# Feed-forward activations transposed by VectorE blocks and two DMAs instead of on TensorE, and a bucket table written 32 times instead of 128

## The chip, the cores and the metric

The kernel runs on one core of a Trainium2 chip. The metric is the device time of one execution in microseconds; lower is better. The trace was taken by the hardware profiler from one execution, and its times count from the first instruction of that execution.

## The reference, cut to what matters

Two transformer blocks run one after the other on one sequence of 256 tokens with 2048 features, in float32. Each ends in a gated feed-forward of width 5632 (the first block's `D_FF` and the second's `D_FF_2`), and these two are what the change touches, besides a bias of the second block's attention:

```python
# first block
gate, up = jnp.split(h @ w_gate_up[layer], 2, axis=-1)
x = x + rms_norm((jax.nn.silu(gate) * up) @ w_down[layer], g_ffn_post[layer])

# second block: a causal convolution of width 3 over the tokens, for each of 2 * 5632 columns
def conv_ffn(h, w_up, conv_w, conv_b, w_down):
    L = h.shape[1]
    u = h @ w_up
    up = jnp.pad(u, ((0, 0), (CONV_WIDTH - 1, 0), (0, 0)))
    acc = conv_b
    for j in range(CONV_WIDTH):
        acc = acc + conv_w[j] * up[:, j:j + L]
    gate, val = jnp.split(acc, 2, axis=-1)
    return (jax.nn.silu(gate) * val) @ w_down

# second block's attention: a bias for each head from the bucket of the distance
dist = t_pos[None, :, None] - sel
bias = t5_table[t5_bucket(jnp.maximum(dist, 0))]
```

## The kernel before

**Matmuls.** Every weight matrix is cut into chunks of 512 output columns, and a chunk into half pieces of 256 rows (512 KB). The 256 tokens are two tiles `t` of 128. A product is made of three float32r passes: activation high part by weight high part (A), high by low (B), low by high (C). So a half piece and a tile make 6 matmuls of 128x128 by 128x512, all issued in `step` (line 331). A chunk over 2048 rows has 8 half pieces and 96 matmuls. Its result stands with tokens on the partitions, in one PSUM bank of the class `mm` for each tile.

**Weights.** SyncE loads a half piece into a staging page (line 254), ScalarE casts it into the high part (line 278), VectorE subtracts for the low part (line 285). Casts are issued up to 12 planned us ahead of the piece's first matmul (`AHEAD_HI`), low parts 11 (`AHEAD_LO`).

**Order.** One Python loop (`run`) writes out the order of the whole program: it walks the matmul steps with a planned clock of 0.216 us for a matmul, and issues loads, casts and low parts as they come due. What happens after a chunk (its `done`) is a generator. All generators move by one tick for every 1.4 planned us (`TICK`, `pump`), and `yield n` sleeps n ticks. Ticks only set the place of an instruction in its engine's queue; each engine works through its queue in order and waits where an operand is missing.

**Memory.** SBUF is 25 pages of 128x2048 floats (`PAGES`), shared by weights (`ring`, `stg`), whole pages (`s8`) and quarter pages of 128x512 (`s2`, at most 4 pages). PSUM has 4 banks of the class `mm` and 4 of `sd`. The DMAs of the generators go out on GpSimd's queue (`mq`), the weight loads on SyncE's.

**First feed-forward** (`ffn`, 11 blocks of 512 columns in parts of two). A gate chunk leaves silu(gate) in a quarter page (`ffn_gate`). After the up chunk, `ffn_up` multiplies PSUM by it on VectorE (line 1017), sleeps 1 + 2 ticks, transposes the 128x512 result on TensorE in four squares into an `sd` bank (line 346), and `evac_split` makes the high part on ScalarE (line 352) and the low part on VectorE (line 353), feature-major, for the down chunks. Chunks of part g + 1 stand ahead of the down chunks of part g, so a block is finished well before it is read, except for the last one: between its up chunk and its own down part stand only the four down chunks of the part before.

**Second feed-forward** (`ffn2`, same order). After each gate or value chunk `two` scales the two tiles out of PSUM on ScalarE (line 1214), and after 3 ticks `conv` transposes them on TensorE, two groups of four squares a tick apart (line 1534), so that tokens lie along the free dimension. On each of four 128x256 pieces ScalarE applies the first tap and the bias (line 1541) and VectorE the two others (lines 1542 and 1543), reading the `sd` bank. A gate's result gets its silu (line 1546). After a value chunk GpSimd multiplies gate by value (line 1560), ScalarE makes the high part (line 1563) and GpSimd the low part (line 1564).

**Bucket table.** `prep_t5`, started at the second gate chunk of the first feed-forward, forms for 8 heads the 512 bias values by distance, with the heads on eight partitions, and writes each head's row 128 times to DRAM (line 490). Much later `topk` reads it with a row step of 511 (line 1284), so that each partition gets a row shifted by one: one DMA for each token tile.

Of the kernel before, what the change touches and what calls it, by code (L numbers as in the profile page):

```python
# [8 lines left out]
F32 = mybir.dt.float32  # L9
# [9 lines left out]
P = 128  # L19
# [17 lines left out]
B_STEP = 2  # L37
LO_LAG = 2
NEG = -1.0e30
EPS = 1e-6  # L40
# [39 lines left out]
class Core:  # L80
# [267 lines left out]
    def evac_split(self, bank, hi, lo, scale=None):  # L348
# [5 lines left out]
        else:  # L354
            nc.scalar.activation(hi, bank, AF.Copy, scale=scale)
            nc.vector.scalar_tensor_tensor(lo, bank, scale, hi.bitcast(F32), op0=ALU.mult, op1=ALU.subtract)

    def x_block(self, src, xt, j, t, goff):

        nc = self.nc  # L360
        if xt.blk[j] is None:
            xt.blk[j] = True
            xt.blk[j] = yield from self.get("s8", dt=F32R)
        while xt.blk[j] is True:
            yield 1
        bank = yield from self.get("sd")
        self.transposes(bank, [src[:, a * P : (a + 1) * P] for a in range(4)])
        g = [self.cols[:, goff + 4 * j + a : goff + 4 * j + a + 1] for a in range(4)]
        b3 = bank.rearrange("p (k n) -> p k n", k=4)
        s = slice(t * P, (t + 1) * P)  # L370
        hi, lo = xt.hi(j)[:, :, s], xt.lo(j)[:, :, s]
        for a in range(4):
            nc.scalar.activation(hi[:, a], b3[:, a], AF.Copy, scale=g[a])  # L373
        xt.ready_hi.add((j, t))

        def low():
            yield LO_LAG
            for a in range(4):
                nc.vector.scalar_tensor_tensor(lo[:, a], b3[:, a], g[a], hi[:, a].bitcast(F32), op0=ALU.mult, op1=ALU.subtract)  # L379
            self.put("sd")  # L380
            xt.ready.add((j, t))

        self.spawn(low())
# [12 lines left out]
    def consts(self):  # L396
# [22 lines left out]
        self.d_lb = d.tile([2, 1024], F32, name="d_lb")  # L419
        self.d_t5 = d.tile([8, P, 512], F32, name="d_t5")  # L420

# [57 lines left out]
    def prep_t5(self):  # L479
        nc, i = self.nc, self.i  # L480
        hot, w = yield from self.get("s2", 2)
        bank = yield from self.get("sd")
        self.mq.dma_start(hot[0:32, :], i["c_hot"])
        self.mq.dma_start(w[0:32, 0:8], i["t5"])
        yield 6
        nc.tensor.matmul(bank[0:8, :], w[0:32, 0:8], hot[0:32, :], start=True, stop=True)
        yield 2
        nc.scalar.copy(w[0:8, :], bank[0:8, :])
        self.put("sd")
        self.mq.dma_start(self.d_t5, w[0:8, None, :].to_broadcast([8, P, 512]))  # L490
        self.drop(hot, w)
        self.flags.add("t5")
# [516 lines left out]
    def ffn_up(self, c, i):  # L1009
# [3 lines left out]
        def done(t):  # L1013
# [5 lines left out]
            a = self.act[i]  # L1019
            yield 1  # L1020
            if a.blk[0] is None:
                a.blk[0] = True
                a.blk[0] = yield from self.get("s8", dt=F32R)
            while a.blk[0] is True:
                yield 1
            yield 2
            bank = yield from self.get("sd")
            self.transposes(bank, [g[:, b * P : (b + 1) * P] for b in range(4)])
            self.drop(g)
            s = slice(t * P, (t + 1) * P)  # L1030
            self.evac_split(bank.rearrange("p (k n) -> p k n", k=4), a.hi(0)[:, :, s], a.lo(0)[:, :, s])
            self.put("sd")
            a.ready.add((0, t))
# [240 lines left out]
    def topk(self):  # L1274
# [7 lines left out]
        for t in range(2):  # L1282
            n = P * (t + 1)
            self.mq.dma_start(bias[t], bass.AP(tensor=self.d_t5.tensor, offset=self.d_t5.offset + 255 - P * t,
                                               ap=[[511, P], [P * 512, 8], [1, n]]))
        for t in range(2):
# [237 lines left out]
    def conv(self, c, i, gate):  # L1524
# [3 lines left out]
        def then(got):  # L1528
            outs = []
            for a in range(2):  # L1530
                bank = yield from self.get("sd")
                for b in range(2):
                    for t in range(2):
                        nc.tensor.transpose(bank[:, (2 * b + t) * P : (2 * b + t + 1) * P],  # L1534
                                            got[t][:, (2 * a + b) * P : (2 * a + b + 1) * P], self.ident)
                o = yield from self.get("s2")
                for b in range(2):
# [5 lines left out]
                    nc.vector.scalar_tensor_tensor(v[:, 2:], u[:, 0:254], w[0], v[:, 2:], op0=ALU.mult, op1=ALU.add)  # L1543
                self.put("sd")
                if gate:
# [3 lines left out]
                yield 1  # L1549
            self.drop(got[0], got[1])  # L1550
            if gate:
# [415 lines left out]
def _layout(np, a):  # L1967
# [5 lines left out]
    def cols(v):  # L1973
        return v.reshape(-1, 128).T

    conv_w = a["conv_w_2"][0]
    vectors = [a["g_mix_pre"][0], a["g_ffn_pre"][0], a["g_ple_pre"][0], a["norm1_g_2"][0], a["norm2_g_2"][0],
               a["kv_norm_g_2"][0], a["hgrn_gnorm"][0], a["conv_b_2"][0], conv_w[0], conv_w[1], conv_w[2]]
    r = {
# [8 lines left out]
        "w_gu": _pieces(np, a["w_gate_up"][0]),  # L1988
        "w_dn": _pieces(np, a["w_down"][0]),
        "w_pg": _pieces(np, a["w_ple_gate"][0]),  # L1990
# [6 lines left out]
        "w_up2": _pieces(np, a["w_up_2"][0]),  # L1997
        "w_dn2": _pieces(np, a["w_down_2"][0]),
        "g_mix_post": a["g_mix_post"][0], "g_ffn_post": a["g_ffn_post"][0], "g_ple_post": a["g_ple_post"][0],
# [20 lines left out]
```

## Time and profile before

| | |
|---|---|
| three runs | 2699.81, 2703.37, 2704.06 us; median 2703.37 |
| the profiled execution | 2698.83 us, span of its instructions 2696.8 us |
| TensorE, matmuls | 2656.7 us busy, 99% |
| VectorE | 1559.6 us, 58% |
| ScalarE | 1310.5 us, 49% |
| GpSimd | 312.5 us, 12% |
| weight queue (SyncE) | 476.83 MB, 51.0% of the 16 DMA engines' time |
| GpSimd's DMA queue | 34.50 MB, 4.2% |

Busy time is the time in which an engine had at least one instruction under way. Matmuls overlap, so the mean duration of one (392 ns at line 331) is longer than the distance between two starts. A group of the trace is named by line, engine, operation and operands; "idle before" is the engine's idle time just ahead of the group's instructions, with what ended it. A line can be that of a helper: line 346 serves all callers of `transposes`.

### The profile page before, as it was taken

The page shows a single profiled execution, that of the slowest core. Times are in us where ns is not written, and L with a number is a line of the kernel's source. Part 1 is how long each engine was busy: PE and PEld are TensorE (multiplying, and loading weights), DVE is VectorE, ACT ScalarE, POOL GpSimd, SP SyncE. Part 2 cuts the span into 40 slices and gives each one's busy share as a digit, 9 for nine tenths or more (in the row PEclk, how much of TensorE's full clock was granted, in tenths as well). Part 3 has the DMA queues.
Part 4 walks back from the last instruction along what each step waited for, and adds up shares of the span by engine and source line. Part 5 has one row for each costly group of instructions (what it writes and reads, how often), then busy time and mean ns, then how long its engine had stood idle before and what let it go on. Part 6 is the DMA issues. An engine that isn't in the chain of part 4 may idle for free. (4 is left out here: it accounts for less than half of the span.)

```text
span 2696.8 us, 32408 instructions
## 1 busy us (share of the span) xinstructions
PE 2656.7 (99%) x12193; PEld 2194.9 (81%) x12193; DVE 1559.6 (58%) x2063; ACT 1310.5 (49%) x1916; POOL 312.5 (12%) x298
## 2 busy tenths in 40 slices
PE   8999999999999999999999999999999999999998
PEld 7887788888778888888887778788888888888887
DVE  6865675465635445454557564855555646464656
ACT  6545644454525443434345564555455535353634
POOL 1341031021200000000002310100001101020101
PEclk9999999999999999999999999999999999999999
DMA  7445446667576555555557555455555555555553
GB/s 252 164 144 165 152 154 200 218 230 262 197 182 227 191 195 193 193 197 193 192 176 241 206 211 179 146 178 198 187 181 189 185 189 185 190 194 181 195 180 132
DMA packets 144539, 513.97 MB, mean 191 GB/s; under 512 B 17688, under 2 KB 20272, under 8 KB 143360
## 3 DMA queue, kind: packets, MB, share of 16 engines
q1 hardware_dynamic: 133504, 476.83, 51.0%
q0 software_dynamic: 9584, 34.50, 4.2%
q8 instruction: 95, 1.56, 0.2%
q10 hardware_dynamic: 1296, 0.59, 0.1%
q14 instruction: 60, 0.49, 0.1%
HBM read 497.16 MB, written 14.70 MB: 190 GB/s over the span
## 5 line engine op out<-in xcount | busy, mean ns | idle before, releaser
L331 PE MATMUL mm<-ring,s 128*128 128x512 f32 (+1 forms) x10824 | 2526.3, 392 | 4.1 <-ACT s L373 4.1
L331 PEld LDWEIGHTS mm<-ring,s 128*128 128x128 f32 x10824 | 2018.8, 188 | 424.2 <-issue 7.1
L285 DVE TENSOR_TENSOR ring<-stg,ring 128x1024 fp32r<-128x1024 f32 x896 | 1090.7, 1263 | 477.8 <-ACT ring L278 469.4
L278 ACT CAST ring<-stg 128x1024 fp32r<-128x1024 f32 (+1 forms) x904 | 905.1, 1050 | 186.0 <-PE mm L331 68.0
L352 ACT CAST s<-sd 128x512 fp32r<-128x512 f32 (+2 forms) x56 | 28.9, 516 | 225.7 <-PE sd L346 187.9
L1214 ACT ACTIVATE s<-mm,ss 128x512 f32<-128x512 f32 x60 | 41.5, 692 | 198.7 <-PE mm L331 186.0
L1051 DVE TENSOR_TENSOR s<-mm,s 128x512 f32<-128x512 f32 x72 | 48.9, 688 | 107.8 <-PE mm L331 107.8
L1560 POOL TENSOR_TENSOR s<-s,s 128x512 f32<-128x512 f32 x22 | 40.5, 1841 | 583.1 <-DVE s L1543 583.1
L1541 ACT ACTIVATE s<-sd,cols 128x256 f32<-128x256 f32 x88 | 48.6, 563 | 96.0 <-DVE s L1543 61.8
L1542 DVE SCALAR_TENSOR_TENSOR s<-sd,cols,s 128x255 f32<-128x255 f32 x88 | 42.4, 482 | 83.0 <-ACT s L1541 82.4
L1017 DVE SCALAR_TENSOR_TENSOR s<-mm,ss,s 128x512 f32<-128x512 f32 x22 | 16.4, 750 | 110.6 <-PE mm L331 110.6
L1004 ACT ACTIVATE s<-mm,ss 128x512 f32<-128x512 f32 x22 | 15.2, 691 | 132.0 <-PE mm L331 130.8
L346 PE MATMUL sd<-ident,s 128*128 128x128 f32 x340 | 54.6, 284 | 21.3 <-DVE s L975 7.2
L346 PEld LDWEIGHTS sd<-ident,s 128*128 128x128 f32 x340 | 43.2, 146 | 36.1 <-issue 10.2
L353 DVE TENSOR_TENSOR s<-sd,s 128x512 fp32r<-128x512 f32 (+2 forms) x56 | 33.9, 605 | 65.6 <-ACT s L352 65.6
L1064 POOL DMA_DIRECT2D s<-in_p_dram x2 | 1.1, 550 | 603.8 <-PE mm L331 603.8
L799 POOL TENSOR_TENSOR s<-s,s 128x512 f32<-128x512 f32 x32 | 53.1, 1668 | 94.0 <-ACT s L796 89.3
L373 ACT ACTIVATE s<-sd,cols 128x128 fp32r<-128x128 f32 x160 | 45.7, 383 | 30.4 <-PE sd L346 27.5
L341 POOL TENSOR_TENSOR small<-small,mhalf 128x1 f32<-128x1 f32 (+1 forms) x27 | 22.3, 825 | 310.7 <-DVE small L340 278.2
L379 DVE SCALAR_TENSOR_TENSOR s<-sd,cols,s 128x128 fp32r<-128x128 f32 x160 | 44.2, 342 | 10.6 <-ACT s L373 10.6
L1543 DVE SCALAR_TENSOR_TENSOR s<-sd,cols,s 128x254 f32<-128x254 f32 x88 | 42.4, 481 | 3.1
L800 DVE TENSOR_TENSOR s<-s,s 128x512 f32<-128x512 f32 x32 | 32.2, 1027 | 11.5 <-ACT s L796 11.5
(290 smaller groups left out, 1121.6 us busy)
## 6 DMA issues: line engine op xcount, KB each, us to landing
stg<-in_w_in_dram SPq DMA_DIRECT2D x232, 512.0 KB, 4.4
stg<-in_w_gu_dram SPq DMA_DIRECT2D x176, 512.0 KB, 5.3
stg<-in_w_dn_dram SPq DMA_DIRECT2D x176, 512.0 KB, 5.2
stg<-in_w_up_dram SPq DMA_DIRECT2D x176, 512.0 KB, 5.0
stg<-in_w_out_dram SPq DMA_DIRECT2D x32, 512.0 KB, 5.4
stg<-in_w_pg_dram SPq DMA_DIRECT2D x32, 512.0 KB, 5.6
stg<-in_w_o_dram SPq DMA_DIRECT2D x32, 512.0 KB, 4.7
stg<-in_w_hb_dram SPq DMA_DIRECT2D x16, 512.0 KB, 4.9
```

The costliest lines, as they stand in the source:

```text
L278: nc.scalar.copy(w[:, 0, :, 0 : cc.n], stg[n_hi][0][:, :, 0 : cc.n])
L285: eng.tensor_tensor(wl[:, :, 0 : cc.n], unstage(n_lo)[:, :, 0 : cc.n], wh[:, :, 0 : cc.n].bitcast(F32), op=ALU.subtract)
L331: nc.tensor.matmul(c.ps[t][:, 0 : c.n], xl if p == "C" else xh, wl if p == "B" else wh, start=n == 0, stop=n == 6 * c.nhp - 1)
L346: self.nc.tensor.transpose(bank[:, a * P : (a + 1) * P], s, self.ident)
L373: nc.scalar.activation(hi[:, a], b3[:, a], AF.Copy, scale=g[a])
L379: nc.vector.scalar_tensor_tensor(lo[:, a], b3[:, a], g[a], hi[:, a].bitcast(F32), op0=ALU.mult, op1=ALU.subtract)
L799: nc.gpsimd.tensor_tensor(k3, d3, kt[:, None, :].to_broadcast([P, 4, P]), op=ALU.mult)
L1051: nc.vector.tensor_tensor(y, ps[t], y, op=ALU.add)
L1214: nc.scalar.activation(r, ps[t], AF.Copy, scale=self.rs[t])
L1541: nc.scalar.activation(v, u, AF.Identity, scale=w[2], bias=self.cols[:, C_CB + k : C_CB + k + 1])
L1542: nc.vector.scalar_tensor_tensor(v[:, 1:], u[:, 0:255], w[1], v[:, 1:], op0=ALU.mult, op1=ALU.add)
L1543: nc.vector.scalar_tensor_tensor(v[:, 2:], u[:, 0:254], w[0], v[:, 2:], op0=ALU.mult, op1=ALU.add)
```

## The change

In `ffn_up` and `conv` the transposes on TensorE go. `flip_out` transposes each 32x32 block of a 128x512 tile on VectorE and writes the result to a DRAM scratch tile (one of eight). `flip_in`, `FLIP_OUT` = 5 ticks later, reads it back with partitions rearranged in runs of 128 floats. `FLIP_IN` = 10 ticks after that the tile is used. The features come out in another order within each 512, and the host reorders the rows of the down weights and the columns of the convolution's weights to match. In `ffn_up` the split into high and low part reads the tile from SBUF. In `conv` ScalarE first copies the two tiles' pieces into one SBUF tile, which takes the place of the PSUM bank. The bucket table is written 32 times for each head instead of 128, and each of its two reads becomes four of 32 partitions.

```diff
+FLIPS = 8
+FLIP_OUT = 5
+FLIP_IN = 10
+    def flip_out(self, src):
+        nc = self.nc
+        ts = yield from self.get("s2")
+        nc.vector.transpose(ts, src)
+        self.drop(src)
+        self.serial += 1
+        d = self.dram.tile([P, 512], F32, tag="flip", bufs=FLIPS, name=f"flip_{self.serial}")
+        self.mq.dma_start(d, ts)
+        return ts, d
+
+    def flip_in(self, d):
+        tr = yield from self.get("s2")
+        self.mq.dma_start(tr.rearrange("p (i x) -> p i x", i=4), d.rearrange("(i r) (j x) -> (r j) i x", i=4, j=4))
+        return tr
...
-        self.d_t5 = d.tile([8, P, 512], F32, name="d_t5")
+        self.d_t5 = d.tile([8, 32, 512], F32, name="d_t5")
...
-        self.mq.dma_start(self.d_t5, w[0:8, None, :].to_broadcast([8, P, 512]))
+        self.mq.dma_start(self.d_t5, w[0:8, None, :].to_broadcast([8, 32, 512]))
...
@@ ffn_up
-            yield 1
+            ts, d = yield from self.flip_out(g)
+            yield FLIP_OUT
+            tr = yield from self.flip_in(d)
+            self.drop(ts)
...
-            yield 2
-            bank = yield from self.get("sd")
-            self.transposes(bank, [g[:, b * P : (b + 1) * P] for b in range(4)])
-            self.drop(g)
+            yield FLIP_IN
             s = slice(t * P, (t + 1) * P)
-            self.evac_split(bank.rearrange("p (k n) -> p k n", k=4), a.hi(0)[:, :, s], a.lo(0)[:, :, s])
-            self.put("sd")
+            hi, lo = (z[:, :, s].rearrange("p a (i q) -> p a i q", q=32) for z in (a.hi(0), a.lo(0)))
+            self.evac_split(tr.rearrange("p (i a q) -> p a i q", i=4, a=4), hi, lo)
+            self.drop(tr)
...
@@ topk
-            self.mq.dma_start(bias[t], bass.AP(tensor=self.d_t5.tensor, offset=self.d_t5.offset + 255 - P * t,
-                                               ap=[[511, P], [P * 512, 8], [1, n]]))
+            for b in range(4):
+                self.mq.dma_start(bias[t][32 * b : 32 * b + 32],
+                                  bass.AP(tensor=self.d_t5.tensor, offset=self.d_t5.offset + 255 - P * t - 32 * b,
+                                          ap=[[511, 32], [32 * 512, 8], [1, n]]))
...
@@ conv
-            outs = []
+            outs, ds, trs = [], [], []
+            for t in range(2):
+                ds.append((yield from self.flip_out(got[t])))
+            yield FLIP_OUT
+            for ts, d in ds:
+                trs.append((yield from self.flip_in(d)))
+                self.drop(ts)
+            yield FLIP_IN
             for a in range(2):
-                bank = yield from self.get("sd")
-                for b in range(2):
-                    for t in range(2):
-                        nc.tensor.transpose(bank[:, (2 * b + t) * P : (2 * b + t + 1) * P],
-                                            got[t][:, (2 * a + b) * P : (2 * a + b + 1) * P], self.ident)
-                o = yield from self.get("s2")
+                bank, o = yield from self.get("s2", 2)
+                b4 = bank.rearrange("p (b t i q) -> p b t i q", b=2, t=2, i=4)
+                for t in range(2):
+                    nc.scalar.copy(b4[:, :, t], trs[t].rearrange("p (i a q) -> p a i q", i=4, a=4)[:, 2 * a : 2 * a + 2])
```

## Rows read from the trace of the kernel before

**Rows 1.** The page's engine table: busy us, share of the span, instructions.
```profile
span 2696.8 us, 32408 instructions
PE 2656.7 (99%) x12193; PEld 2194.9 (81%) x12193; DVE 1559.6 (58%) x2063; ACT 1310.5 (49%) x1916; POOL 312.5 (12%) x298
```

**Rows 2.** The page's costliest group: busy us, mean ns, idle us before it, releaser.
```profile
L331 PE MATMUL mm<-ring,s 128*128 128x512 f32 (+1 forms) x10824 | 2526.3, 392 | 4.1 <-ACT s L373 4.1
```

**Rows 3.** Busy us by engine, clock, DMA share, GB/s: the two feed-forward stretches.
```profile
760.00:1440.00 680.00, 677.46 (x3019) 559.66 (x3019) 335.68 (x328) 268.36 (x303) 9.24 (x13) 1.00 0.58 195
1947.00:2677.00 730.00, 730.00 (x3310) 604.65 (x3310) 425.88 (x497) 360.48 (x455) 78.40 (x52) 1.00 0.53 183
```

**Rows 4.** TensorE's timeline, second feed-forward: start us, us, instructions.
```profile
1973.37 0.60 PE L1534 MATMUL sd<-ident,s 128*128 128x128 f32 x4
...
1996.07 0.60 PE L1534 MATMUL sd<-ident,s 128*128 128x128 f32 x4
```

**Rows 5.** TensorE's timeline, first feed-forward; in brackets the idle us before, with releaser.
```profile
801.54 0.76 PE L346 MATMUL sd<-ident,s 128*128 128x128 f32 x4 [2.54 <-DVE s L1017]
...
805.36 42.45 PE L331 MATMUL mm<-ring,s 128*128 128x512 f32 x186
847.66 0.60 PE L346 MATMUL sd<-ident,s 128*128 128x128 f32 x4
...
849.83 42.45 PE L331 MATMUL mm<-ring,s 128*128 128x512 f32 x186
892.11 0.60 PE L346 MATMUL sd<-ident,s 128*128 128x128 f32 x4
```

**Rows 6.** The chain of waits in order of time: start us, us, what.
```profile
1973.53 0.44 PE sd L1534 x4
```

**Rows 7.** DMA issues, KB each, median us to landing: 750 to 810, then whole run.
```profile
stg<-in_w_gu_dram SPq DMA_DIRECT2D x17, 512.0 KB, 20.5
d_t<-s POOLq DMA_DIRECT2D x1, 2048.0 KB, 46.1
...
stg<-in_w_gu_dram SPq DMA_DIRECT2D x176, 512.0 KB, 5.3
```

**Rows 8.** Timeline of GpSimd and ScalarE after the bucket table.
```profile
762.96 1.10 POOL L490 DMA_DIRECT2D d_t<-s  x1 [30.62 <-ACT s L488]
...
786.11 1.05 ACT L278 CAST ring<-stg 128x1024 fp32r<-128x1024 f32 x1 [5.55 <-DMA stg<-in_w_gu_dram]
```

**Rows 9.** The view of rows 3 for the 20 us around the stop.
```profile
800.00:820.00 20.00, 18.46 (x79) 15.25 (x79) 12.60 (x13) 9.30 (x10) 0.00 (x0) 0.91 0.79 261
```

**Rows 10.** DMAs of GpSimd's queue: issue ns min/median/max of line 1284; KB, landing us.
```profile
L1284 POOL DMA_DIRECT2D s<-d_t x2: 897/932/967, 1665.2 to 1667.9; - x2
...
d_gate<-s POOLq DMA_DIRECT2D x16, 256.0 KB, 2.6
s<-d_t POOLq DMA_DIRECT2D x1, 512.0 KB, 5.5
```

**Rows 11.** Groups by shape of line and engine, as rows 2, nearest to the added work.
```profile
L285 DVE TENSOR_TENSOR ring<-stg,ring 128x1024 fp32r<-128x1024 f32 x888 | 1084.2, 1267 | 475.5 <-ACT ring L278 467.1 <-issue 7.8
L1541 ACT ACTIVATE s<-sd,cols 128x256 f32<-128x256 f32 x88 | 48.6, 563 | 96.0 <-DVE s L1543 61.8 <-PE sd L1534 34.2
L1339 ACT ACTIVATE s<-s,small 128x256 f32<-128x256 f32 x16 | 8.0, 502 | 3.6 <-DVE small L1334 3.6
L1583 DVE TENSOR_TENSOR s<-s,s 128x512 f32<-128x512 f32 x8 | 5.5, 692 | 3.5 <-ACT s L1580 3.4
```

**Rows 12.** GpSimd's timeline at a value chunk's products, the first and the last.
```profile
2000.11 2.11 POOL L1560 TENSOR_TENSOR s<-s,s 128x512 f32<-128x512 f32 x1 [46.67 <-DVE s L1543]
...
2007.90 1.29 POOL L1564 TENSOR_TENSOR s<-s,s 128x512 fp32r<-128x512 f32 x1 [0.73 <-ACT s L1563]
```

**Rows 13.** Timeline of the last block: its last product, the last part's first sum.
```profile
2636.01 1.31 POOL L1564 TENSOR_TENSOR s<-s,s 128x512 fp32r<-128x512 f32 x1 [0.73 <-ACT s L1563]
...
2668.83 0.69 DVE L1577 TENSOR_TENSOR s<-mm,s 128x512 f32<-128x512 f32 x1 [1.66 <-PE mm L331]
```

More of the change, by code (lines that the diff above doesn't have):

```diff
@@ L1543, in then @@
                     nc.vector.scalar_tensor_tensor(v[:, 2:], u[:, 0:254], w[0], v[:, 2:], op0=ALU.mult, op1=ALU.add)
-                self.put("sd")
+                self.drop(bank)
                 if gate:
@@ L1549, in then @@
                 yield 1
-            self.drop(got[0], got[1])
+            self.drop(*trs)
             if gate:
@@ L1974, in cols, with flip @@
         return v.reshape(-1, 128).T
-    conv_w = a["conv_w_2"][0]
+    def flip(w):
+        return np.ascontiguousarray(w.reshape(-1, 4, 4, 32, *w.shape[1:]).swapaxes(1, 2).swapaxes(2, 3)).reshape(w.shape)
+    conv_w = flip(a["conv_w_2"][0].T).T
     vectors = [a["g_mix_pre"][0], a["g_ffn_pre"][0], a["g_ple_pre"][0], a["norm1_g_2"][0], a["norm2_g_2"][0],
-               a["kv_norm_g_2"][0], a["hgrn_gnorm"][0], a["conv_b_2"][0], conv_w[0], conv_w[1], conv_w[2]]
+               a["kv_norm_g_2"][0], a["hgrn_gnorm"][0], flip(a["conv_b_2"][0]), conv_w[0], conv_w[1], conv_w[2]]
     r = {
@@ L1988, in _layout @@
         "w_gu": _pieces(np, a["w_gate_up"][0]),
-        "w_dn": _pieces(np, a["w_down"][0]),
+        "w_dn": _pieces(np, flip(a["w_down"][0])),
         "w_pg": _pieces(np, a["w_ple_gate"][0]),
@@ L1997, in _layout @@
         "w_up2": _pieces(np, a["w_up_2"][0]),
-        "w_dn2": _pieces(np, a["w_down_2"][0]),
+        "w_dn2": _pieces(np, flip(a["w_down_2"][0])),
         "g_mix_post": a["g_mix_post"][0], "g_ffn_post": a["g_ffn_post"][0], "g_ple_post": a["g_ple_post"][0],
```

## The prediction

> **What bounds the kernel now.** I read the engine table first: TensorE is busy 2656.7 of 2696.8 us [rows 1]. Busy time alone proves little, so I looked next at the idle time ahead of the weight matmuls of line 331: 4.1 us in all, before 10,824 of them [rows 2]. Then I read both feed-forward stretches, where nearly all of the change lies: TensorE is busy 677.5 of 680 us in the first and 730.0 of 730 us in the second, at a granted clock of 1.00, with VectorE busy 336 and 426 us of it, ScalarE 268 and 360, GpSimd 9 and 78, and the DMA engines at 0.58 and 0.53 [rows 3]. The reader should see one full queue beside four half empty ones: what leaves TensorE's stream shortens the kernel, and what is put elsewhere is free while it comes in time.
>
> **Transposes taken from TensorE.** The change removes 4 transposes in each of 22 calls of the first feed-forward (11 blocks, 2 token tiles) and 8 in each of 22 calls of the second (11 gates, 11 values): 88 + 176 = 264, in 66 groups of four. A transpose lasts 272 ns in the trace, but the four overlap, so the duration isn't the price. I price a group from start to start. In the second stretch one chunk of 96 matmuls and two groups takes 1973.37 to 1996.07 = 22.70 us [rows 4]. A run of 186 matmuls without transposes takes 805.36 to 847.66 = 42.30 us, 0.2274 each [rows 5]; 96 of these are 21.83, so two groups cost 0.87. In the first stretch two chunks (192 matmuls, two groups) take 847.66 to 892.11 = 44.45 [rows 5], less 192 x 0.2274 = 43.66: 0.79. That makes 22 x 0.87 + 11 x 0.79 = 27.8 us. The chain of waits gives 0.44 to a group [rows 6], so 66 x 0.44 = 29.0. I take 28.5, between them.
>
> The Trainium skill speaks against the move: "VectorE: DVE Perf Modes", section "Rules for kernel authors", wants a 128x128 transpose on TensorE where PSUM will do as its destination. By engine time that agrees with the rows below (0.44 us there, about 0.69 on VectorE), but the rule does not ask which engine is full.
>
> **The bucket table.** The old kernel writes 2048 KB from eight partitions and the write takes 46.1 us to land; weight loads in that stretch land after a median of 20.5 us against 5.3 over the run [rows 7]. ScalarE waits for weights, 5.55 us before one cast [rows 8], each late cast delays VectorE's low halves, VectorE's line 1017 stands in order behind these, and TensorE's transposes wait 2.54 us for it [rows 5]. After that stop the clock is granted at 0.91 over 800 to 820 us [rows 9], where it is 1.00 over either feed-forward [rows 3]: TensorE, having stood still, runs for a while at 1.2 instead of 2.4 GHz. The pair of groups that takes 847.66 to 849.83 = 2.17 us elsewhere takes 801.54 to 805.36 = 3.82 here, 1.65 more [rows 5]. So this write costs 2.54 + 1.65 = 4.2 us. A quarter of the bytes at the same rate is 11.5 us; ScalarE's first wait came 23 us after the issue (762.96 to 786.11) [rows 8], so stock covers it. I count all 4.2 us; bounds 0 (if another cause starved these loads) and 4.2. The reads of the table become 8 DMAs instead of 2, six more issues of at most 0.97 us [rows 10] on GpSimd's queue, which has all of the selection on VectorE to do them in: nothing, at worst 6 us if the table came last there.
>
> **What is added, and what hides it.** VectorE gets 66 block transposes of 128x512. None is in the trace. The nearest row is an SBUF operation of that size, 0.69 us, which I take; the ends are 0 (an added instruction can't give time back) and the 1.27 us of an operation of twice the size [rows 11]. At 0.69 the second stretch gets 44 x 0.69 = 30 us on 426 busy of 730: 62%. Conv's multiplies now read SBUF instead of PSUM; no row has that form, and I expect no change; VectorE has some 270 us to spare there either way. ScalarE gets 88 copies of 128x256 at 0.50 us, the row of that size from SBUF, bounds 0 and the 0.56 out of PSUM [rows 11]: 44 us on 360 of 730, 55%. None reaches TensorE by load; zero, with 0 to 5 us kept in the range.
>
> GpSimd gets 66 writes and 66 reads of 256 KB. A write like that, to the gate scratch, lands in 2.6 us. The read has runs of 512 B; the nearest row is the table's 512 KB read in 512-byte runs, 5.5 us, with 0.90 to 0.97 us on GpSimd to issue it [rows 10]. So a read lands in 3 to 6 us. Writes and reads add a megabyte to each chunk of the second feed-forward, where weights bring four: the DMA share goes from 0.53 to about 0.66.
>
> **The waits that are added.** The read waits on GpSimd's queue for its write; behind it stand the products of lines 1560 and 1564. The split (first feed-forward) and the copies (second) wait on ScalarE's queue for the read; behind them stand the weight casts that TensorE lives on. The schedule puts 5 ticks between write and read and 10 between read and use. A tick is 1.4 planned us; a chunk planned at 96 x 0.216 = 20.7 took 21.8 without its transposes, so ticks are 1.47 us: 7.4 and 14.7 us. The worst case is a gate chunk, whose read is queued behind the products of the value chunk ahead: these hold GpSimd from 2000.11 to 2009.19, 9 us [rows 12]. They start about 20 ticks after their chunk's end and the read is due at 22.8, so it slips by about 6 us: 6 + 2 of issuing + 5.5 is 13.5 of 14.7 us. ScalarE waits 0, at worst 2 or 3 us, and casts are issued 12 us ahead of use. I take nothing.
>
> At the end of the second feed-forward the cover is thin. Today the last block is ready at 2636.01 + 1.31 = 2637.3. The last part's first 12 matmuls end at 2668.8, so it is needed from 2668.8 - 12 x 0.2274 = 2666.1 [rows 13], about 0.9 earlier once the groups ahead are gone. Fifteen ticks (22 us) and four copies (2 us) later it is ready at 2661.4: 4 us in hand, less what ScalarE loses there to casts that wait. 0 to 3 us; I take 0.5.
>
> **Sum.** 28.5 + 4.2 - 0.5 = 32.2 us. The profiled execution took 2698.83 (span 2696.8 and 2.0 around it), so 2666.6 for one like it. The median of the three runs, 2703.37, lies 4.5 higher; from it 2671.2. I forecast 2670.
>
> **The rivals.**
> 1. *A new small wait takes part of the gain* (read late by a few us in gate chunks, the last block late, or the table's 4.2 us not returned): 5 to 18 us kept back, 2675 to 2688. For it: the 1 us margin behind the products and the 4 us at the end. Against: casts run 12 us ahead.
> 2. *Slower: the reads land so late that ScalarE stands still with the casts behind it.* Place: the split or copies of each of 33 pairs of tiles. With some 10 us of lead absorbed, each us beyond it costs 33 us; the gain is gone when ScalarE is held about 11 us per pair, that is when a pair lands 26 us after its issue. At 13 us held TensorE loses about 3 us a pair, 99 us less the 32: 2770; at 12 us, 2737. For it: the table's write shows that this queue can starve the weights for 46 us. Against: that came from eight partitions, and the 512 KB read with equal runs landed in 5.5 us. The Trainium skill has a rule for this side ("VectorE: DVE Perf Modes", section "The three transpose paths"): a plain DMA that transposes by strides is 19 times slower than the crossbar's when its innermost destination stride is large. By it a read of 256 KB would be an estimated 52 us (19 halves of the row's 5.5), and this rival would hold many times over. Here the innermost run is 512 contiguous bytes on both sides, and the row of 5.5 us speaks against it; its chance is part of this rival's.
> 3. *Nothing moves: the weights' path is the true limit*, TensorE only seems full, and the time it is spared returns as waits for casts: within 5 us of today, 2698 to 2708. For it: ScalarE already waits for weights near 786 us [rows 8]. Against: 4.1 us of idle ahead of 10,824 matmuls, and a constant 0.227 us each.
> 4. *More is gained than the transposes' slots* (matmuls next to a group are late too): 2655 to 2662.
>
> **How the numbers follow.** Forecast (2662 to 2675) 0.70, rival 1 0.15, rival 2 0.08, rival 3 0.05, rival 4 0.02. The range 2661 to 2688 takes in the forecast and rival 1. This kernel's measurement tells 0.2%, 5.4 us, from no change. Faster: 0.70 + 0.15 + 0.02 = 0.87; same 0.05; slower 0.08.
>
> **What would show it.** Right: no group of lines 346 or 1534 in the feed-forwards; an up chunk every 21.8 us instead of 22.7; TensorE without idle near 800 us and the table landing in about 12 us; reads landing in 3 to 6 us; VectorE near 1610 busy. Wrong: TensorE idle ahead of line 331 with casts as releaser at the copies (rival 2); chunks that still take 22.7 us (rival 3); a gap at the end of the second feed-forward (rival 1). What would undo the forecast is a block transpose or a read several times dearer than its nearest row.

## The result, and the profile after

| | before | after |
|---|---|---|
| median of 4 runs each, us | 2703.72 | 2671.02 |
| lowest to highest, us | 2699.81 to 2705.5 | 2669.01 to 2673.43 |
| profiled execution, us | 2698.83 | 2673.43 |
| its span, us | 2696.8 | 2671.6 |

The changed kernel takes 0.9881 of the time of the one before (95% interval 0.9864 to 0.9899): 32.7 us less by the medians. The two profiled executions differ by only 25.4 us, because the one of before was quicker than any of the four timed runs and the one of after was the longest of its four. So I read stretches inside the traces against each other, and take whole times from the medians.

The page of the changed kernel, engine table, costliest group and the four groups that matter for the added work (columns as in [rows 1, 2]):

```profile
span 2671.6 us, 32470 instructions
...
PE 2629.4 (98%) x11929; PEld 2171.5 (81%) x11929; DVE 1618.9 (61%) x2129; ACT 1340.6 (50%) x2004; POOL 401.0 (15%) x436
...
L334 PE MATMUL mm<-ring,s 128*128 128x512 f32 (+1 forms) x10824 | 2511.2, 392 | 6.5 <-ACT s L393 4.7
...
L369 POOL DMA_DIRECT2D flip<-s x66 | 37.0, 561 | 991.3 <-DVE s L365 985.6
...
L375 POOL DMA_DIRECT2D s<-flip x66 | 50.4, 765 | 62.9 <-DMA flip<-s 42.6
...
L355 ACT CAST s<-s 128x512 fp32r<-128x512 f32 x22 | 13.5, 618 | 74.4 <-DMA s<-flip 68.7
...
L365 DVE STREAM_TRANSPOSE s<-s 128x512 f32<-128x512 f32 x66 | 46.2, 706 | 1.6
```

TensorE has 264 instructions fewer (12193 to 11929) and is still the full queue: 6.5 us of idle ahead of 10,824 weight matmuls, where it was 4.1 [rows 2]. Line 331 is line 334 now. The new idle time is on other engines: GpSimd's reads (line 375) wait 42.6 us for their writes, and ScalarE's split in the first feed-forward (line 355) waits 68.7 us for reads.

The two feed-forward stretches and the 20 us after the bucket table's write, as in [rows 3, 9]:

```profile
760.00:1420.00 660.00, 660.00 (x2911) 545.43 (x2910) 347.01 (x344) 268.50 (x296) 32.71 (x51) 1.00 0.61 214
1930.00:2655.00 725.00, 725.00 (x3204) 600.34 (x3203) 479.00 (x549) 388.45 (x547) 134.69 (x141) 1.00 0.64 220
800.00:820.00 20.00, 20.00 (x90) 16.55 (x89) 12.55 (x13) 0.62 (x1) 2.66 (x4) 1.00 0.70 256
```

VectorE goes from 426 busy of 730 to 479 of 725 in the second stretch, GpSimd from 78 to 135, the DMA share from 0.53 to 0.64, and TensorE is as full as before. Around 800 us it no longer stops, and the clock stays at 1.00 where it was 0.91 [rows 9].

What a chunk costs now is read from ScalarE's first scaling of each value and gate chunk (line 1235; start us, us, instructions, idle before):

```profile
1986.91 0.69 ACT L1235 ACTIVATE s<-mm,ss 128x512 f32<-128x512 f32 x1 [12.86 <-PE mm L334]
...
2008.67 0.69 ACT L1235 ACTIVATE s<-mm,ss 128x512 f32<-128x512 f32 x1 [3.81 <-PE mm L334]
...
2030.43 0.69 ACT L1235 ACTIVATE s<-mm,ss 128x512 f32<-128x512 f32 x1 [1.26 <-PE mm L334]
```

Two steps of 21.76 us, where the one in [rows 4] was 22.70: 0.94 for two groups of transposes, or 0.47 for one.

The DMAs of GpSimd's queue, KB each and median us to landing, as in [rows 7, 10]:

```profile
flip<-s POOLq DMA_DIRECT2D x66, 256.0 KB, 2.6
s<-flip POOLq DMA_DIRECT2D x66, 256.0 KB, 5.9
...
d_t<-s POOLq DMA_DIRECT2D x1, 512.0 KB, 12.9
```

To compare kernels by stage I take two intervals from each trace. The second feed-forward is counted from the last matmul stretch of the output projection to the first sum of the last part. The first is counted from the first weight matmul after the stage ahead of it to VectorE's normalization behind it (line 975, now 995). In the rows of e_in_20, e_in_8, e_in_6, e_gap_5_4 and e_close, where stops of TensorE or a late VectorE shift that first sum, the second column is 719.0 plus what the same weight matmuls come later on TensorE by the end of the stage. Microseconds, of the profiled execution of each kernel that was run below:

| kernel | median | first | second |
|---|---|---|---|
| before | 2702.87 to 2704.45 | 720.8 | 739.7 |
| after | 2671.02 | 707.4 | 719.0 |
| e_after_again | 2670.22 | 708.3 | 719.0 |
| e_pe_back | 2700.55 | 718.7 | 739.8 |
| e_second_only | 2680.82 | 718.2 | 719.0 |
| e_table_128 | 2673.70 | 712.3 | 719.0 |
| e_table_only | 2700.83 | 718.7 | 739.7 |
| e_in_20 | 2676.58 | 707.6 | 726.5 |
| e_in_8 | 2672.10 | 707.7 | 723.2 |
| e_in_6 | 2709.04 | 707.9 | 759.3 |
| e_gap_5_4 | 2738.63 | 707.5 | 789.1 |
| e_gap_1_14 | 2687.02 | 724.6 | 721.2 |
| e_close | 2820.23 | 720.8 | 853.4 |

What stands outside these two varies by a few us from execution to execution of the same kernel (before the first feed-forward: 698.5 us in after, 694.2 in e_after_again), so the stages tell apart what medians only bound.

### The profile page after: what moved, and what is told of

Its sections match the earlier page's. It is cut to its first block, busy times and chain, and to the rows that moved or that the text cites. A ratio compares the mean times of both kernels' runs of the same rounds, so it can differ in the third digit from the quotient of the medians.

```text
span 2671.6 us, 32470 instructions
## 1 busy us (share of the span) xinstructions
PE 2629.4 (98%) x11929; PEld 2171.5 (81%) x11929; DVE 1618.9 (61%) x2129; ACT 1340.6 (50%) x2004; POOL 401.0 (15%) x436
## 5 line engine op out<-in xcount | busy, mean ns | idle before, releaser
L369 POOL DMA_DIRECT2D flip<-s x66 | 37.0, 561 | 991.3 <-DVE s L365 985.6
L349 PE MATMUL sd<-ident,s 128*128 128x128 f32 x252 | 42.3, 292 | 21.1 <-DVE s L995 8.7
L393 ACT ACTIVATE s<-sd,cols 128x128 fp32r<-128x128 f32 x160 | 45.8, 382 | 32.2 <-PE sd L349 29.4
L349 PEld LDWEIGHTS sd<-ident,s 128*128 128x128 f32 x252 | 33.0, 150 | 33.2 <-DVE s L995 8.2
L375 POOL DMA_DIRECT2D s<-flip x66 | 50.4, 765 | 62.9 <-DMA flip<-s 42.6
L355 ACT CAST s<-sd 64x256 fp32r<-64x256 f32 (+2 forms) x34 | 16.0, 471 | 86.3 <-PE sd L349 49.1
L356 DVE TENSOR_TENSOR s<-s,s 128x512 fp32r<-128x512 f32 x22 | 15.2, 690 | 64.6 <-ACT s L355 64.3
L355 ACT CAST s<-s 128x512 fp32r<-128x512 f32 x22 | 13.5, 618 | 74.4 <-DMA s<-flip 68.7
L1569 ACT ACTIVATE s<-s,cols 128x256 f32<-128x256 f32 x88 | 48.2, 595 | 1.5
L365 DVE STREAM_TRANSPOSE s<-s 128x512 f32<-128x512 f32 x66 | 46.2, 706 | 1.6
```

Of the source, the lines that this page charges most:

```text
L349: self.nc.tensor.transpose(bank[:, a * P : (a + 1) * P], s, self.ident)
L365: nc.vector.transpose(ts, src)
L375: self.mq.dma_start(tr.rearrange("p (i x) -> p i x", i=4), d.rearrange("(i r) (j x) -> (r j) i x", i=4, j=4))
L1569: nc.scalar.activation(v, u, AF.Identity, scale=w[2], bias=self.cols[:, C_CB + k : C_CB + k + 1])
```

## The experiments

My theory: TensorE's queue is what is full, so each group of transposes is worth its slot there, and the schedule hides the added work. Rival: the gain comes from somewhere else (the table, the SBUF sources), or the hiding is chance. The first five kernels split the gain; the other six ask what the hiding rests on.

**e_after_again** is the changed kernel unaltered, for the spread.

> The changed kernel unaltered, timed again as the yardstick of this batch. Theory (the gain is the TensorE slots of 66 groups, 28.5 us, and the stall at the bucket table, 4.2 us): 31 to 35 us below the kernel before, ratio 0.988. Its trace is a second look at what lies outside the feed-forwards: in the first trace of the changed kernel the first feed-forward's transposes began 5.9 us later than before (698.5 against 692.65) with no edit ahead of them. If that is chance from run to run, this trace shows another offset; if the change causes it (another placing of tiles), it shows the same 5 to 6 us.

2670.22 us, 0.9879 (0.9865 to 0.9892). The second feed-forward came out at 719.0 twice; the 4 us between the two spans (2671.6 and 2667.7) lie ahead of the first feed-forward.

**e_pe_back** keeps all that the change adds, and puts the 264 transposes back on TensorE as idle work, on the tile that VectorE has transposed, with nobody reading their result. The cut shows the edit in `ffn_up`; `conv` gets two such groups, a tick apart, ahead of its reads.

```diff
+            bank = yield from self.get("sd")
+            self.transposes(bank, [ts[:, b * P : (b + 1) * P] for b in range(4)])
+            self.put("sd")
             tr = yield from self.flip_in(d)
...
```

> The changed kernel with the 264 TensorE transposes put back as idle work: each tile that VectorE has transposed is also transposed on TensorE in a group of four, five ticks later, into a bank that nobody reads. Theory (the price is the slots, 0.40 to 0.45 us a group): 27 to 30 us slower than the changed kernel, 3 to 7 us faster than the kernel before. Rival (the slots were covered, and what was gained is the wait of those transposes and what hung on it): within 5 us of the changed kernel.

2700.55 us, 0.9988 (0.9979 to 0.9996): 30.3 us more than the changed kernel beside it, 0.46 for each of 66 groups. The detour is still there, its reads and copies too; what it brought is gone. So the gain is TensorE's slots, and the added work by itself costs nothing that can be seen: the second feed-forward takes 739.8 with the transposes and the detour together, and 739.7 in the kernel before.

**e_second_only** leaves the first feed-forward as it was before, with its transposes, and changes only the second.

```diff
-            ts, d = yield from self.flip_out(g)
-            yield FLIP_OUT
-            tr = yield from self.flip_in(d)
+            yield 1
...
-            yield FLIP_IN
+            yield 2
+            bank = yield from self.get("sd")
+            self.transposes(bank, [g[:, b * P : (b + 1) * P] for b in range(4)])
...
```

> The changed kernel with the first feed-forward as before the change (22 groups back on TensorE, the split out of PSUM) and the rest as changed. By the slots: 22 x 0.40 to 0.45 = 8.7 to 9.9 us slower than the changed kernel, 22 to 24 us faster than the kernel before. If the first feed-forward's transposes cost more there than their slots (they stand behind VectorE's line): 12 us slower or more.

2680.82 us, 10.6 more than the changed kernel: 0.48 for each of 22 groups, where I expected 8.7 to 9.9 us. The price is the same in both stages.

**e_table_128** is the changed kernel with the bucket table written 128 times again; **e_table_only** is the kernel before with the table written 32 times.

```diff
-        self.d_t5 = d.tile([8, 32, 512], F32, name="d_t5")
+        self.d_t5 = d.tile([8, P, 512], F32, name="d_t5")
...
-        self.mq.dma_start(self.d_t5, w[0:8, None, :].to_broadcast([8, 32, 512]))
+        self.mq.dma_start(self.d_t5, w[0:8, None, :].to_broadcast([8, P, 512]))
...
```

> The changed kernel with the bucket table written 128 times again (2048 KB, two reads). Theory (the write starves the weights for 46 us, and TensorE runs dry whoever is first in its queue): 2 to 6 us slower than the changed kernel, TensorE idle for some 2 us near 800 us, clock below 1.00 there. Rival (only the transposes behind VectorE's line had to wait, and the matmuls' stock would have lasted): no difference, TensorE without a gap near 800 us though weight loads land in about 20 us.

> The kernel before with nothing but the bucket table written 32 times and read in eight pieces. By the stall as priced: 4.2 us faster than the kernel before, no idle time of TensorE ahead of the transposes near 800 us, the write landing in 12 to 13 us. Rival (the stall moves to another wait): within 2 us.

e_table_128 takes 2673.70 us, 3.5 more; its first feed-forward takes 4.0 more than that of e_after_again. Its TensorE timeline and the window:

```profile
813.72 51.53 PE L334 MATMUL mm<-ring,s 128*128 128x512 f32 x219 [2.63 <-DVE ring L288]
```
```profile
800.00:820.00 20.00, 17.37 (x70) 13.88 (x70) 11.38 (x12) 9.33 (x9) 2.66 (x4) 0.91 0.78 247
```

The reader should see the stop of [rows 5] again, 2.63 us instead of 2.54, though no transposes stand in this stretch: now the weight matmuls themselves wait for VectorE's low parts, and the clock falls to 0.91 as in [rows 9]. It comes 43 weight matmuls further on than in the kernel before, so it is a stop of the same kind and size and not the same one: there the transposes met it first.

e_table_only takes 2700.83, 0.9988 (0.9979 to 0.9997): 2.5 us less than before, with an interval from 0.8 to 5.7, where I expected 4.2. TensorE has no stop near 800 us in it. Medians are a blunt tool for this, and TensorE's timeline settles it. From the last transposes for the first feed-forward's input to a pair near its end stand the same 2,892 weight matmuls and the same transposes in both kernels; first before, then with the table alone:

```profile
720.64 0.60 PE L346 MATMUL sd<-ident,s 128*128 128x128 f32 x4
...
1393.59 0.38 PE L346 MATMUL sd<-ident,s 128*128 128x128 f32 x2
```
```profile
722.49 0.60 PE L346 MATMUL sd<-ident,s 128*128 128x128 f32 x4
...
1391.09 0.38 PE L346 MATMUL sd<-ident,s 128*128 128x128 f32 x2
```

672.95 us against 668.60: the table is worth 4.35 us on TensorE. Between the same weight matmuls e_table_128 takes 4.2 more than e_after_again. The column above shows only 2.1 of it (720.8 to 718.7), because that stage ends behind the last load of the normalization's weights. GpSimd issued this load 2.5 us earlier in e_table_only (1428.72 against 1431.22), but it was used 6.0 us after its issue began, against 3.7 in the profiled execution of before and 5.0 to 6.0 in the eleven other traces. So 2.3 us went there.

**e_close** takes the cover away: read one tick after the write, use one tick after the read.

```diff
-FLIP_OUT = 5
-FLIP_IN = 10
+FLIP_OUT = 1
+FLIP_IN = 1
```

> The changed kernel with the steps close together: FLIP_OUT 1 instead of 5 and FLIP_IN 1 instead of 10, so ScalarE's split and copies stand 2 ticks behind VectorE's transposes and wait for write and read, about 9 to 12 us for a pair. The mechanism of the slow rival as it was priced (10 us of lead absorbed, each us beyond it 33 us): 0 to 70 us slower than the changed kernel, with TensorE idle ahead of the weight matmuls. If the lead is larger than priced (in the changed kernel one split held ScalarE for 13.3 us and TensorE had no gap): within 5 us of it, with over 200 us of ScalarE waiting for the read in its trace.

2820.23 us, 1.0431 (1.0416 to 1.0445): 150 us more than the changed kernel, 117 more than before. Both expectations failed (0 to 70 us, or within 5). Its waits (total us, times, longest), and its costliest group:

```profile
ACT s L355 <- DMA s<-flip: 258.3, 22, 21.9
ACT s L1564 <- DMA s<-flip: 233.4, 44, 12.2
```
```profile
L334 PE MATMUL mm<-ring,s 128*128 128x512 f32 (+1 forms) x10824 | 2564.6, 396 | 93.2 <-DVE ring L288 79.2
```

This is rival 2, made on purpose: ScalarE held, the casts behind it late, VectorE's low parts after them, and TensorE without weights. The windows of both stages:

```profile
760.00:1440.00 680.00, 672.50 (x2942) 551.47 (x2941) 349.77 (x347) 270.65 (x305) 35.04 (x56) 0.99 0.60 209
1960.00:2790.00 830.00, 744.66 (x3073) 598.71 (x3072) 454.06 (x526) 384.84 (x528) 137.27 (x140) 0.94 0.54 189
```

The price is uneven. In the first feed-forward ScalarE is held 23.5 us per pair of tiles (258.3 over 11) and the stage is 12.5 us longer. In the second it is held 10.6 us per call (233.4 over 22) and the stage is 134 longer: TensorE stands idle for 85 us of the window, and the clock is granted at 0.94 instead of 1.00, so part of the time it runs at 1.2 instead of 2.4 GHz after its stops.

**e_gap_5_4** cuts the second wait from ten ticks to four, **e_gap_1_14** moves the first one's ticks behind the read.

```diff
-FLIP_IN = 10
+FLIP_IN = 4
```

> The changed kernel with FLIP_IN 4 instead of 10: 9 ticks in all, 13 us. In the run with the steps close ScalarE was held 10.6 us in each of the 22 calls of conv and the second feed-forward took 134 us longer, 6.1 us a call; in the first one it was held 23.5 us a pair and lost 12.5 us in all. Theory (a hold is paid above a lead of about 4 to 5 us in the second feed-forward, where conv's own 10 us of copies, taps and silu stand behind it, and above some 20 in the first): ScalarE held 1 to 4 us a call, within 8 us of the changed kernel. Rival (there is no lead: each us held is paid at the rate of the close run, 0.58): 22 calls of 1 to 4 us cost 13 to 50 us.

```diff
-FLIP_OUT = 5
-FLIP_IN = 10
+FLIP_OUT = 1
+FLIP_IN = 14
```

> The changed kernel with FLIP_OUT 1 and FLIP_IN 14: the same 15 ticks from VectorE's transpose to the use, but the read follows its write at once on GpSimd's queue. Theory (only ScalarE's hold counts, and GpSimd may wait for the write as nothing urgent stands behind the read): within 5 us of the changed kernel, GpSimd waiting for writes some 130 us as in the run with the steps close, ScalarE waiting no more than in the changed kernel. Rival (the wait on GpSimd's queue is the harm of the close steps): a good part of the 150 us lost there is lost here, 20 us or more.

Both expectations failed. e_gap_5_4 takes 2738.63 us (1.0130, 1.0116 to 1.0144), 68 more than the changed kernel. ScalarE's copies wait 205.0 us for reads, 9.3 in each of 22 calls, where nine ticks at 1.47 us should have left 1 to 4. Its timeline at one call:

```profile
2018.91 0.68 ACT L1235 ACTIVATE s<-mm,ss 128x512 f32<-128x512 f32 x1
2019.49 5.78 ACT L281 CAST ring<-stg 128x1024 fp32r<-128x1024 f32 x6
...
2032.34 0.40 ACT L1564 COPY s<-s 128x256 f32<-128x256 f32 x1 [7.07 <-DMA s<-flip]
2034.23 0.41 ACT L1564 COPY s<-s 128x256 f32<-128x256 f32 x1 [1.48 <-DMA s<-flip]
```

Ticks are an order, not a time. A chunk is 20.7 planned us, 14.8 ticks of 1.4. In the changed kernel the copies come 3 + 5 + 10 = 18 ticks after their chunk's scaling (3 in `two`, then FLIP_OUT and FLIP_IN) and stand on ScalarE's queue behind the next chunk's scaling (line 1235), which waits for TensorE. That wait holds ScalarE back to TensorE's time, and the read has landed by then. The changed kernel's ScalarE at the same place:

```profile
2030.43 0.69 ACT L1235 ACTIVATE s<-mm,ss 128x512 f32<-128x512 f32 x1 [1.26 <-PE mm L334]
...
2031.96 0.69 ACT L1235 ACTIVATE s<-mm,ss 128x512 f32<-128x512 f32 x1
...
2033.48 0.71 ACT L1564 COPY s<-s 128x256 f32<-128x256 f32 x2
```

With FLIP_IN = 4 they come at 12 ticks, ahead of the next scaling. Nothing on the queue then ties ScalarE to TensorE; it runs through its casts, arrives early by the lead that they have, and stands still.

e_gap_1_14 takes 2687.02 us (0.9940, 0.9927 to 0.9952), 16.8 more. The second feed-forward loses only 2.2 of it; the first loses 16, at two places of TensorE's timeline:

```profile
768.36 1.86 PE L506 MATMUL sd<-s 32*8 32x512 f32 x2 [7.92 <-DMA s<-in_t_dram]
...
1385.73 0.54 PE L349 MATMUL sd<-ident,s 128*128 128x128 f32 x2 [3.81 <-DMA s<-in_p_dram]
```

These are small loads for TensorE that stand on GpSimd's queue behind a read that waits for its write. GpSimd's timeline ahead of the first stop:

```profile
763.91 0.76 POOL L375 DMA_DIRECT2D s<-flip  x1 [6.94 <-DMA flip<-s]
...
765.18 0.50 POOL L504 DMA_DIRECT2D s<-in_t_dram  x1
```

Over the whole run the reads wait 130.3 us for their writes, where it was 42.6. I had named the products behind that read and no loads. The wait for `in_t_dram` is in e_close as well (5.11 us).

**e_in_6, e_in_8, e_in_20** test the order against the clock: the copies come at 14, 16 and 28 ticks, against 14.8 for a chunk.

```diff
-FLIP_IN = 10
+FLIP_IN = 8
```

> The changed kernel with FLIP_IN 8 instead of 10. With 4 the second feed-forward took 71 us longer. Two theories of why. Place in the queue: a chunk is 20.74 planned us, 14.8 ticks; conv's copies stand 3 + 5 + FLIP_IN ticks after their chunk. At 18 they stand behind the scaling of the next chunk's result out of PSUM (line 1235), which ties ScalarE to TensorE's time; at 12 they stand ahead of it, ScalarE reaches them early by the lead of its casts, and is held 9.3 us. At 16 they stand behind it still: within 5 us of the changed kernel, ScalarE waiting under 3 us a call. Time from tick to tick: each tick less takes 1.5 us from the read, and from FLIP_IN 10 to 4 cost 11 us a tick: 2 ticks cost 15 to 30 us.

> The changed kernel with FLIP_IN 6. Place in the queue: 3 + 5 + 6 = 14 ticks, ahead of the next chunk's scaling in every call: 35 to 65 us slower than the changed kernel, ScalarE held 6 to 9 us a call, and a jump of at least 30 us between FLIP_IN 8 and 6. Time from tick to tick: 45 us slower, half way and no jump: FLIP_IN 8 loses about 23.

> The changed kernel with FLIP_IN 20. It tests the cover at the end of the second feed-forward: in the changed kernel the last block's last product ends at 2632.6 and the last part needs it at 2643.8 - 12 x 0.2267 = 2641.1, 8.5 us later. Ten ticks more are 14.7 us: TensorE stands idle about 6 us there, 5 to 9 us slower than the changed kernel with the clock's dip; in the first feed-forward 35 ticks of 1.4 planned us against 41.5 planned us until the block is read: no loss. If the copies' place matters elsewhere (28 ticks, just ahead of the second next chunk's end at 29.6), ScalarE meets a read that landed long ago: no loss.

By the medians all three came as expected, e_in_8 and e_in_6 by the place in the queue. e_in_8 takes 2672.10 us (0.9878), as the changed kernel; e_in_6 takes 2709.04 (1.0013, 1.0001 to 1.0025), 37 us more for two ticks. The waits of the copies, first with 8 ticks, then with 6:

```profile
ACT s L1564 <- DMA s<-flip: 26.9, 14, 2.9
```
```profile
ACT s L1564 <- DMA s<-flip: 161.0, 42, 8.7
```

Two ticks are some 3 us; the hold goes from 1.2 to 7.3 us a call. That is the step of an order and not of a time. The traces show the order itself: the copies stand behind both scalings of the next chunk in 17 of 22 calls with 10 ticks and with 8; with 6 they stand behind one of the two in 2 calls and behind none in the other 20. Eight ticks are not quite free, though. In the profiled execution of e_in_8 the second feed-forward loses 4.2 us at one place, in three stops of TensorE of 0.8 to 1.0 us, of which these are the first two:

```profile
2105.84 3.24 PE L334 MATMUL mm<-ring,s 128*128 128x512 f32 x12 [0.81 <-DVE ring L288]
2110.09 3.25 PE L334 MATMUL mm<-ring,s 128*128 128x512 f32 x12 [1.01 <-DVE ring L288]
```

Sent the other way, e_in_20 takes 2676.58 us, 6 more: the last block is late, and TensorE stops for it.

```profile
2635.36 0.74 PE L334 MATMUL mm<-ring,s 128*128 128x512 f32 x2 [0.80 <-ACT s L1591]
2636.72 1.19 PE L334 MATMUL mm<-ring,s 128*128 128x512 f32 x4 [0.62 <-POOL s L1592]
2639.91 1.22 PE L334 MATMUL mm<-ring,s 128*128 128x512 f32 x2 [2.00 <-ACT s L1591]
2641.47 3.78 PE L334 MATMUL mm<-ring,s 128*128 128x512 f32 x8 [0.34 <-POOL s L1592]
```

The stops are 3.8 us of the 7.5 that its second feed-forward loses. Over the ten us from 2640 on the clock is granted at 0.70 (last but two of the columns), between the levels of 1.2 and 2.4 GHz:

```profile
2640.00:2650.00 10.00, 9.66 (x30) 7.31 (x31) 3.66 (x6) 1.45 (x4) 3.57 (x5) 0.70 0.33 106
```

With this the changed kernel's 10 lies between two ends, 8 and 20, and no version tried beats it.

## Why the prediction was right, point by point

**The bound.** Right. TensorE was the full queue, the time went down by its slots, and e_pe_back gave them back.

**The groups: 28.5 us, measured 30.3.** The mechanism was right and the size 6% low. The second feed-forward went from 739.7 to 719.0: 20.7 us for 44 groups, 0.47 each; e_second_only gives 0.48 in the first. I had 0.40 to 0.45. The low term is the matmul that I subtracted, in both stretches. I took 0.2274 us from a run whose ends lie against groups [rows 5], so it holds some of the groups' own price. A chunk without transposes takes 21.76 us, 0.2267 each, and in the changed kernel's first stretch the matmuls follow each other at 0.2267 too. With that [rows 4] hold 22.70 - 21.76 = 0.94 for two groups where I had 0.87, and [rows 5] hold 44.45 - 192 x 0.2267 = 0.92 where I had 0.79. The chain's 0.44 [rows 6] is low too.

**The table: 4.2 us, measured 4.2 and 4.35 on TensorE (2.5 and 3.5 by medians).** Right in kind and in size: the stop and the low clock are gone with the new table alone and back with the old one. One step was too narrow: I had the cost at the transposes' wait for VectorE's line 1017, and e_table_128 shows such a stop without transposes, where the weights themselves run out. The write lands in 12.9 us; I had 11.5. ScalarE's wait for weights [rows 8] ended 23 us after the issue of the old write and had begun at 786.11 - 5.55 = 780.56, 17.6 us after it, which still covers a write of 12.9.

**The sum: 32.2 us, measured 32.7.** That it came so close is in part luck. In the changed kernel the stretch of 2,892 weight matmuls above takes 658.30 us (726.55 to 1384.85), 14.65 less than before: 4.35 for the table and 10.3 for 22 groups. With the 20.7 of the second feed-forward TensorE gains 35.4 us in the two profiled executions. The medians give 32.7, with an interval of 27 to 37 us, and what stands outside the two stages varies by as much as they differ.

**The hidden work.** The block transpose takes 0.706 us (0.69 was taken) and ScalarE's copy 0.41 (0.50). The read lands in 5.9 (3 to 6), its issue takes 0.77 (0.90 to 0.97). VectorE stands at 66% of the second stretch instead of 62%, since the convolution's multiplies take some 20 us more in all, which I had not expected; the first of them before, and its commonest form after:

```profile
L1542 DVE SCALAR_TENSOR_TENSOR s<-sd,cols,s 128x255 f32<-128x255 f32 x88 | 42.4, 482 | 83.0 <-ACT s L1541 82.4
```
```profile
L1570 DVE SCALAR_TENSOR_TENSOR s<-s,cols 128x255 f32<-128x255 f32 x52 | 31.4, 603 | 20.1 <-ACT s L1569 20.0
```

The mean of 603 ns hides two kinds. Of the 176 multiplies 155 take 0.48 us out of SBUF, as they did out of PSUM, so my "no change" held for the operation. The other 21 take 1.1 to 1.6 us, and they make up the 20 us. Each of them runs beside a product of GpSimd that had begun before it or within 0.02 us of it, and ends 0.3 us behind that product; VectorE's and then GpSimd's timeline at one place:

```profile
2019.49 0.48 DVE L1570 SCALAR_TENSOR_TENSOR s<-s,cols,s 128x255 f32<-128x255 f32 x1
2020.01 1.48 DVE L1571 SCALAR_TENSOR_TENSOR s<-s,cols,s 128x254 f32<-128x254 f32 x1
```
```profile
2019.92 1.28 POOL L1592 TENSOR_TENSOR s<-s,s 128x512 fp32r<-128x512 f32 x1 [1.15 <-ACT s L1591]
```

In the kernel before 24 multiplies out of PSUM ran beside such products, and none took more than 0.49. It touched nothing here, as VectorE still has 246 us of that stretch idle.

**The waits.** Here the number was right by luck and the step behind it wrong. I turned ticks into time, found 13.5 of 14.7 us, and called the margin 1 us (by its own figures the read slips by 9.1 - 2.8 x 1.47 = 5 us and not 6, which leaves 2). The copies do not wait for reads in the changed kernel:

```profile
L1564 ACT COPY s<-s 128x256 f32<-128x256 f32 x88 | 31.4, 406 | 21.1 <-DVE s L365 19.9 <-DVE s L1571 0.8 <-ACT ring L281 0.4
```

But that is because of their place behind line 1235, and not by that sum; the same sum gave the miss of e_gap_5_4. In the first feed-forward ScalarE waits up to 13.3 us for a read, 68.7 in all, where I had 0 and at worst 3. ScalarE's timeline there, and VectorE's transpose of the same tile:

```profile
812.32 0.62 ACT L355 CAST s<-s 128x512 fp32r<-128x512 f32 x1 [13.27 <-DMA s<-flip]
823.12 0.69 ACT L1024 ACTIVATE s<-mm,ss 128x512 f32<-128x512 f32 x1 [10.17 <-PE mm L334]
823.70 0.61 ACT L355 CAST s<-s 128x512 fp32r<-128x512 f32 x1
```
```profile
802.14 0.71 DVE L365 STREAM_TRANSPOSE s<-s 128x512 f32<-128x512 f32 x1
```

The first tile's split stands ahead of the next instruction that waits for TensorE (line 1024), the second behind it. ScalarE was at the first at 812.32 - 13.27 = 799.05, 3 us before VectorE began to transpose the tile, and waited until the read was there. TensorE lost nothing, since the casts were that far ahead.

**Rival 2's point of decision.** I put it at 11 us held per pair, with 10 us of lead absorbed. In the second feed-forward it is lower: e_in_6 is held 7.3 us a call and has lost the whole gain (40.3 us over 22 calls, 1.8 each); 9.3 us cost 3.2 a call in e_gap_5_4, 10.6 cost 6.1 in e_close. So some 4.5 to 6 us are absorbed there. In the first, 23.5 us per pair in e_close cost at most 1.1. One number for both stages was the mistake. The read itself was never the danger: 5.9 us in the middle, 8.0 at the longest. The Trainium skill states its factor of 19 ("VectorE: DVE Perf Modes", section "The three transpose paths") against the crossbar's transpose and for a large innermost destination stride. The read here writes contiguous runs of 512 bytes, so the factor was not tested; my estimate of 52 us also put a plain read in the crossbar's place.

**The end.** I had 4 us in hand and charged 0.5. The last product and the last part's first sum in the changed kernel:

```profile
2631.08 1.51 POOL L1592 TENSOR_TENSOR s<-s,s 128x512 fp32r<-128x512 f32 x1 [0.73 <-ACT s L1591]
```
```profile
2643.79 0.69 DVE L1605 TENSOR_TENSOR s<-mm,s 128x512 f32<-128x512 f32 x1 [0.88 <-PE mm L334]
```

Ready at 2632.6, needed at 2643.8 - 12 x 0.2267 = 2641.1: 8.5 us in hand and nothing lost.

**Rivals 1, 3 and 4** did not come. The 5 to 18 us of rival 1 are there with other gaps (16.8 in e_gap_1_14, 6 in e_in_20), in the one case at a place that I had not named, in the other at the end as named.

## What to carry to other kernels

Where one engine is full, price what leaves it by its start-to-start slot over a whole stage, and prove it by leaving the new work in and putting the old back as idle work. What an in-order queue hides depends on what stands ahead of the waiting instruction there: behind one that is tied to the slow engine it costs nothing, and one place ahead of it the queue's whole lead turns into waiting. Before a wait is put on a queue, list all that stands behind it, small loads too.

## What the runs showed of the hardware

- A multiply-add of VectorE for 128x254 or 128x255 took 0.48 us, with its tile in SBUF as with it in PSUM. Out of SBUF it took 1.1 to 1.6 us where a product of GpSimd had begun before it or with it (21 of 176 in the changed kernel), and kept its 0.48 where it had begun ahead of the product (11). The 24 out of PSUM beside such products in the kernel before took 0.47 to 0.49.
- The issue of a DMA by GpSimd took 0.56 us for the write of a 128x512 tile and 0.77 for the read of the same 256 KB in 512-byte runs. The landing is not set by the pattern alone: the median is 2.6 us for the write and 5.9 for the read in the changed kernel, and 5.5 and 3.3 in e_close.
- A block transpose of 128x512 on VectorE costs about what a plain operation of that size does there, 0.706 against 0.692 [rows 11].
- Stops cost TensorE more than their idle time: 2.63 us in e_table_128 went with 4.2 us lost (granted clock 0.91 over 20 us), 3.8 us in e_in_20 with 7.5 (0.70 over ten us), and 2.8 us in three pieces in e_in_8 with 4.2, though the granted clock was 1.00 from 2100 to 2120 us there.
